# Plain float32 products for the first S5 layer's input and gate projections in a hybrid trunk

## The chip, the cores and the metric

The kernel runs on one core of one Trainium2 chip. The metric is device microseconds of one execution. The engines are TensorE (PE: matmuls, and PEld: its weight loads), VectorE (DVE), ScalarE (ACT), GpSimd (POOL) and SyncE (SP, which here only issues DMAs). TensorE's clock is granted by a throttle; the profile shows it as a share of its full 2.4 GHz.

## The reference

One inference step of a trunk of four layers: S5, retention, Hyena, S5. There are 128 context tokens and 256 latent tokens, T = 384 together, and 1024 features. Each layer is a normalisation with a modulation (shift, scale, gate computed from the condition vector with a weight of 1024 x 3072 per layer), a mixer, and a gated residual add. The change concerns the first S5 layer:

```python
def s5_branch(h, h0, w_in, ..., w_glu, b_glu, w_out):
    proj = h @ w_in                          # 1024 -> 2048
    u, gate = proj[..., :S5_WIDTH], proj[..., S5_WIDTH:]
    y = d_skip * uf + <both directions of the scan over u, 64 groups of 16 channels>
    g = jax.nn.gelu(y)
    y = g * jax.nn.sigmoid(g @ w_glu + b_glu)
    out = (y * jax.nn.silu(gate)) @ w_out
```

All inputs and outputs are float32.

## The kernel before

Activations lie feature-major: 8 blocks of 128 features by 384 tokens. A dense product is a loop over slabs of weight (1024 x 256 numbers, 1 MB), each of two blocks of 128 output features, each of which sums over the 8 input blocks: 8 positions of 128x128x384 to an output block. The input projection of layer 0 has four slabs (64 positions), and the gate projection four (slabs 4 to 7 of the same weight, 64 positions).

Precision comes from a split. `unit` (L158) makes from a raw weight block (tile `wr`) a high part `wh` by a cast on ACT (L164) and the rest `wl` by a subtraction, which `sub_any` (L146) deals to POOL (through L136) or DVE (L151) by a counter and the current share. Activations are split likewise into `hh` and `hl` by `put` (L176: cast L177, subtraction L178). `mm` (L138) then issues three products for each position, high by high, high by low and low by high, each in a reduced float32 type. If its operands come unsplit, it issues one plain float32 product.

The raw weights of all these products come through one pool of two buffers (`weight`, L153, tag `wr`), loaded over SP's queue. The modulation weights of the coming layers use the same two buffers: each layer has 12 slabs of 1 MB, and a unit (`mod_unit`, L369, its products at L381) loads one and multiplies it by the condition vectors. Units are queued and taken one by one by `tick` (L355) between other work.

The S5 layer (`s5`, L701) goes through a list of steps written as a string:

```python
PLAN0 = "A7 U0 T1 U1 T1 P0 A9 T1 P1 A11 T1 U2 T1 P2 A13 T1 P3 A15 T1 R0 U3 T1 P4 T1 A16 P5 T1 T1 P6 P7 R1"
```

U is one slab of the input projection (its result goes through memory into tile `U`, L769 and L770). A builds scan weights ahead on DVE from small tables (`gen_b1`, L642; L631, L632, L636). For six of the sixteen blocks this also builds a weight `CP` that is needed later and spilled to memory: two DVE products per direction (L631, L632), an adding DMA from POOL's queue (L634) and a store from that queue (L650); one buffer serves all six, so one spill's build waits for the store of the spill before. P (`use_p`, L742) multiplies `U` by the built scan weights (L749) and transposes (L758). R is the recurrence over chunks (L795 to L798 on DVE, R0 and R1 for two halves of the groups). T is a tick.

After the plan the gate projection follows, held back until the last product of the last P has been issued. Then the groups: the kernel matrices are loaded from memory in eight small DMAs each (tile `Tt`, L852) and transposed (L857), products of `U` and of the recurrence's states `X` give y (L884), and GELU follows. The result is split into `g_parts` (`gh`, `gl`), which the GLU projection reads. A tile scheduler that simulates times fixes the order of each engine's instructions from this program and from the pools.

Of the kernel before, what the change touches and what calls it, by code (L numbers as in the profile page):

```python
# [10 lines left out]
F32 = mybir.dt.float32  # L11
F32R = mybir.dt.float32r
# [6 lines left out]
NB = D // 128  # L19
# [88 lines left out]
def hybrid_trunk(ctx: ExitStack, tc: tile.TileContext, I, O, dbg=None, layers=(0, 1, 2, 3)):  # L108
# [62 lines left out]
    def parts_tile(pool, nb, name):  # L171
        if not SPLIT:
            return [pool.tile([128, nb, T], F32, name=name)]
        return [pool.tile([128, nb, T], F32R, tag=name + s, name=name + s) for s in ("h", "l")]
# [5 lines left out]
    def featmajor(raw, act, nkb, epi, base=0):  # L180
        for m in range(raw.shape[2] // 128):
            ps = psd()
            for k0 in range(0, nkb, NB):
                w = unit(raw[:, k0:k0 + NB, m * 128:(m + 1) * 128])
                for kb in range(NB):
                    mm(ps[:, :T], [p[:, kb, :] for p in w], [a[:, k0 + kb, :] for a in act],
                       k0 + kb == 0, k0 + kb == nkb - 1)
            epi(base + m, ps[:, :T])
# [171 lines left out]
    def drain():  # L360
        tick(len(bg))

    macc = [None, True]

    def settle():
        while not macc[1]:
            tick()

    def mod_unit(i, s, pool=None):  # L369
        if pool is None:  # L370
            raw = weight(I["mod_w"][i, s])
        else:
            raw = load(pool, "wm", I["mod_w"][i, s], tag="wm")
        u, g = s % 4, s // 4
        if u == 0:
            macc[0] = psn()
        ps, macc[1] = macc[0], u == 3
        for k2 in range(2):
            for q in range(4):
                kb = q * 2 + k2  # L380
                TE.matmul(ps[q * 32:(q + 1) * 32, :256], sg[:, kb, 6 - 2 * u:38 - 2 * u], raw[:, kb, :],  # L381
                          start=u == 0 and k2 == 0, stop=u == 3 and k2 == 1)
        if u < 3:
            return
        row = tmp.tile([128, 256], F32, tag="mrow", name="mrow", bufs=1)
        S.copy(row, ps[:, :256])
        for b in range(2):
            TE.matmul(ps[:, 256 + 8 * b:264 + 8 * b], row[:, b * 128:(b + 1) * 128], sel, start=True, stop=True)
        if g == 0:
            MODS[i] = tuple(cst.tile([128, n, 2], F32, name=f"{nm}{i}") for nm, n in (("mod", 24), ("sc", NB), ("gt", NB)))  # L390
        m, sc, gt = MODS[i][:3]
        mb = vec[:, V_MODB + i * 24 + 8 * g:V_MODB + i * 24 + 8 * g + 8].rearrange("p (u b) -> p b u", b=2)
        V.tensor_add(m[:, 8 * g:8 * g + 8, :].rearrange("p (u b) r -> p b u r", b=2),
                     ps[:, 256:272].rearrange("p (b u r) -> p b u r", b=2, u=4),
                     mb.unsqueeze(3).to_broadcast([128, 2, 4, 2]))
        if g == 1:
            V.scalar_tensor_tensor(sc, m[:, 8:16, :], 1.0,
                                   vec[:, V_G + i * 8:V_G + i * 8 + 8].unsqueeze(2).to_broadcast([128, NB, 2]),
                                   op0=OP.add, op1=OP.mult)
            MODS[i] += (True,)  # L400
        if g == 2:
            V.tensor_scalar(gt, m[:, 16:24, :], GT_F[i], None, op0=OP.mult)
# [50 lines left out]
    def adanorm(i, actp, eng=V):  # L453
        m, sc, gt = MODS[i][:3]
        rb, marks = rstd_bcast()
        h = parts_tile(actp, NB, "h")
        early = EARLY.get(i)
        if early:
            early.rb, early.marks = rb, marks
        for fb in range(NB):  # L460
            t = t384("ht")
            mul = V.tensor_mul(t, (early.x[fb] if early else xT[:, fb, :])[:, :T], rb[:, :T])
            if fb == AM:
                ADA[0] = mul.ins
            if early:
                for v, (a, b) in enumerate(SEGS):
                    hi, bias = h[0][:, fb, a:b], m[:, fb, v:v + 1]
                    if fb in HP:
                        G.tensor_scalar(hi, t[:, a:b], bias, None, op0=OP.add)
                    else:  # L470
                        S.activation(hi, t[:, a:b], AF.Identity, bias=bias)
                    V.scalar_tensor_tensor(h[1][:, fb, a:b], t[:, a:b], bias, hi.bitcast(F32), op0=OP.add, op1=OP.subtract)  # L472
                continue
            f = t384("hf")
            for v, (a, b) in enumerate(SEGS):
                S.activation(f[:, a:b], t[:, a:b], AF.Identity, scale=sc[:, fb, v:v + 1], bias=m[:, fb, v:v + 1])
            put(h, fb, f, eng=eng)
        return h

    class Early:  # L480
# [220 lines left out]
    def s5(i, j, nxt, begun=lambda: None):  # L701
# [28 lines left out]
        PBs = {}  # L730
        mark = [None]
        if j == 0:
            grot = mk(eP, "s5g", 2)

        def get_p(hb):
# [75 lines left out]
        for op in (PLAN0, PLAN1)[j].split():  # L811
# [13 lines left out]
            else:  # L825
                tick(n)
        pool_share[0] = PSG
        eP.close()
        if j == 0:
            eT.close()  # L830
# [8 lines left out]
        if j == 1:  # L839
            while gates:  # L840
                gates.popleft()()
        g_parts = [hpool.tile([128, NB, T], F32R, tag="h" + q, name="g" + q) for q in "hl"]
        e2 = ExitStack()
        rot = mk(e2, "s5c", 2)
        Tms = {}
# [732 lines left out]
```

## Time and profile before

| | us |
|---|---|
| median of 3 runs | 1631.56 (1630.19 to 1633.90) |
| profiled execution | 1632.28 |
| its span in the trace | 1630.5 |
| busy PE / DVE / ACT / POOL | 1449.2 / 1246.0 / 692.2 / 664.3 |
| mean granted clock | 0.951 |

The profile is of one execution; its own time is 1.8 us above its span and 0.7 us above the median. Layer 0 takes the first quarter of it. The busy times are sums over stages of very different limits, so what follows is read stage by stage: windows of busy time, and in each the instructions that start late.

### The profile page before, as it was taken

Reading aid. Unit: us, or ns where it says so; the run is one execution under the profiler, and the core shown is the slowest. Engines: PE = TensorE matmul, PEld = TensorE weight load, DVE = VectorE, ACT = ScalarE, POOL = GpSimd, SP = SyncE. Lnnn points to the kernel's source line nnn. Section 1 sums busy time; section 2 is a strip of 40 time slices with the busy share of each in tenths; the row PEclk is TensorE's granted clock in tenths of the full one; section 3 lists DMA queues with packets and bytes.
Section 4 is the critical chain, followed back from the end, with each engine's and each line's share of the span. In section 5 each row is a group of like instructions: output and inputs, shape, how many; then the busy total and the mean of one; then the engine's idle time right before and its main releaser. Section 6 shows DMA issues by size and latency. Waiting matters only on the chain. (4 is left out here: it accounts for less than half of the span.)

```text
span 1630.5 us, 27608 instructions
## 1 busy us (share of the span) xinstructions
PE 1449.2 (89%) x10370; PEld 1280.7 (79%) x10370; DVE 1246.0 (76%) x2935; ACT 692.2 (42%) x1275; POOL 664.3 (41%) x484
## 2 busy tenths in 40 slices
PE   6778787798799899999979999999999999988996
PEld 3555585577588888889968988999998898767886
DVE  8966998699886767755968887888888874379565
ACT  2434522244333333334445544546445534542443
POOL 2111242325374857551225665655666332132221
PEclk9887899899799999999989999999999999999998
DMA  9487499843555555543333322322322345577531
GB/s 359 130 260 224 150 222 253 284 178 128 216 173 179 183 207 187 183 154 130 127 125 101 101 78 75 101 84 95 100 78 94 106 174 201 167 217 196 199 130 65
DMA packets 107805, 261.39 MB, mean 160 GB/s; under 512 B 28535, under 2 KB 68568, under 8 KB 88088
## 3 DMA queue, kind: packets, MB, share of 16 engines
q1 hardware_dynamic: 80768, 200.12, 37.2%
q0 software_dynamic: 11984, 34.87, 7.7%
q10 hardware_dynamic: 14920, 24.65, 4.3%
q8 instruction: 82, 1.34, 0.3%
q14 instruction: 51, 0.42, 0.1%
HBM read 220.37 MB, written 30.83 MB: 154 GB/s over the span
## 5 line engine op out<-in xcount | busy, mean ns | idle before, releaser
L136 POOL TENSOR_TENSOR wl<-wr,wh 128x1024 fp32r<-128x1024 f32 (+2 forms) x99 | 248.9, 2515 | 300.2 <-ACT wh L164 273.6
L164 ACT CAST wh<-wr 128x1024 fp32r<-128x1024 f32 (+4 forms) x211 | 215.7, 1028 | 315.0 <-PE psd L141 200.5
L141 PE MATMUL psd<-hh,wh 128*128 128x384 f32 x880 | 307.3, 350 | 13.5 <-DVE X L798 7.0
L141 PE MATMUL psd<-hl,wh 128*128 128x384 f32 x880 | 305.7, 347 | 6.4 <-DVE hl L472 6.2
L141 PE MATMUL psd<-hh,wl 128*128 128x384 f32 x880 | 305.3, 347 | 4.7 <-POOL wl L136 2.6
L151 DVE TENSOR_TENSOR wl<-wr,wh 128x1024 fp32r<-128x1024 f32 (+3 forms) x112 | 147.2, 1315 | 71.9 <-ACT wh L164 71.5
L141 PEld LDWEIGHTS psd<-hh,wh 128*128 128x128 f32 x880 | 169.7, 193 | 26.6 <-issue 14.5
L141 PEld LDWEIGHTS psd<-hl,wh 128*128 128x128 f32 x880 | 169.9, 193 | 15.9 <-DVE hl L472 8.9
L141 PEld LDWEIGHTS psd<-hh,wl 128*128 128x128 f32 x880 | 169.7, 193 | 12.2 <-issue 5.1
L141 PE MATMUL psd<-wl,hh 128*128 128x256 f32 x384 | 110.0, 288 | 4.0 <-POOL wl L136 2.0
L141 PE MATMUL psd<-wh,hh 128*128 128x256 f32 x384 | 110.0, 292 | 2.6 <-ACT k L1077 1.6
L141 PE MATMUL psd<-wh,hl 128*128 128x256 f32 x384 | 109.0, 286 | 0.0
L381 PE MATMUL psn<-wr,sgc 128*32 128x256 f32 x640 | 58.3, 460 | 35.0 <-DMA wr<-in_mod_w_dram 23.9
L141 PE MATMUL psd<-zb,wh 128*128 128x384 f32 x240 | 80.9, 338 | 0.0
L141 PEld LDWEIGHTS psd<-wl,hh 128*128 128x128 f32 x384 | 74.1, 193 | 6.3 <-POOL wl L136 3.2
L141 PEld LDWEIGHTS psd<-wh,hh 128*128 128x128 f32 x384 | 73.3, 193 | 4.5 <-ACT k L1077 2.0
L636 POOL TENSOR_TENSOR BP<-BP,xt 128x512 f32<-128x512 f32 x32 | 47.3, 1479 | 71.9 <-DVE xt L632 36.4
L141 PEld LDWEIGHTS psd<-wh,hl 128*128 128x128 f32 x384 | 74.1, 193 | 0.1
L631 DVE TENSOR_TENSOR CP<-B,xc 128x512 f32<-128x512 f32 x52 | 52.9, 1044 | 26.5 <-DMA scratch_cpd_dram<-CP 15.6
L632 DVE TENSOR_TENSOR xt<-BI,xc 128x512 f32<-128x512 f32 x52 | 47.2, 909 | 29.6 <-POOL CP L636 17.2
L381 PEld LDWEIGHTS psn<-wr,sgc 128*32 128x32 f32 x640 | 20.0, 124 | 56.9 <-DMA wr<-in_mod_w_dram 27.8
L797 DVE TENSOR_TENSOR X<-X,m 128x64 f32<-128x64 f32 x184 | 64.2, 349 | 0.0
(385 smaller groups left out, 3843.1 us busy)
## 6 DMA issues: line engine op xcount, KB each, us to landing
wr<-in_mod_w_dram SPq DMA_DIRECT2D x40, 1024.0 KB
wr<-in_hy_w_in_dram SPq DMA_DIRECT2D x32, 1024.0 KB
wr<-in_ret_w_in_dram SPq DMA_DIRECT2D x24, 1024.0 KB
wr<-in_s_w_in_dram SPq DMA_DIRECT2D x16, 1024.0 KB
wm<-in_mod_w_dram SPq DMA_DIRECT2D x8, 1024.0 KB
CP<-xt POOLq DMA_DIRECT2D x32, 256.0 KB, 7.2
Tt<-scratch_kd_dram SPq DMA_DIRECT2D x128, 64.0 KB
wr<-in_s_w_glu_dram SPq DMA_DIRECT2D x8, 1024.0 KB
```

What stands on the lines that cost most here:

```text
L136: G.tensor_tensor(out, a, b, op=op)
L141: TE.matmul(out, lhs[a], rhs[b], start=start and i == 0, stop=stop and i == len(combos) - 1)
L151: V.tensor_sub(out, a, b)
L164: S.copy(hi, ap)
L381: TE.matmul(ps[q * 32:(q + 1) * 32, :256], sg[:, kb, 6 - 2 * u:38 - 2 * u], raw[:, kb, :], start=u == 0 and k2 == 0, stop=u == 3 and k2 == 1)
L631: eng.tensor_tensor(out, c1, x[:, 0].unsqueeze(2).to_broadcast([128, 4, 8, 16]), op=OP.mult)
L632: eng.tensor_tensor(t, c2, x[:, 1].unsqueeze(2).to_broadcast([128, 4, 8, 16]), op=OP.mult)
L636: add.tensor_tensor(out, out, t, op=OP.add)
L797: V.tensor_add(dst, dst, m1[:, 0])
```

## The change

For layer 0 the activations `h` become one plain float32 tile (name `hf`, tag `hh`), written directly by ACT, with no `put`. The products of the input and gate projections take the raw weight `wr` as it was loaded, with no `unit`. While the pools of the plan are open (`eP`), modulation units load into a buffer of their own (pool "s5m", tag `wm`, one buffer); afterwards they share `wr` again. The low half of `g_parts` of layer 0 takes its space from another pool. `featmajor` chooses by the number of activation parts, so other layers and the GLU keep their split.

```diff
@@ featmajor
-                w = unit(raw[:, k0:k0 + NB, m * 128:(m + 1) * 128])
+                w = raw[:, k0:k0 + NB, m * 128:(m + 1) * 128]
+                w = unit(w) if len(act) > 1 else [w]
@@
-    macc = [None, True]
+    macc, mpool = [None, True], [None]
@@ mod_unit
+        pool = pool or mpool[0]
         if pool is None:
             raw = weight(I["mod_w"][i, s])
         else:
@@ adanorm
-        h = parts_tile(actp, NB, "h")
+        h = parts_tile(actp, NB, "h") if i else [actp.tile([128, NB, T], F32, tag="hh", name="hf")]
@@
-            f = t384("hf")
+            f = t384("hf") if i else h[0][:, fb, :]
             for v, (a, b) in enumerate(SEGS):
                 S.activation(f[:, a:b], t[:, a:b], AF.Identity, scale=sc[:, fb, v:v + 1], bias=m[:, fb, v:v + 1])
-            put(h, fb, f, eng=eng)
+            if i:
+                put(h, fb, f, eng=eng)
@@ s5
         if j == 0:
+            mpool[0] = mk(eP, "s5m")
             grot = mk(eP, "s5g", 2)
@@
         pool_share[0] = PSG
+        mpool[0] = None
         eP.close()
@@
-        g_parts = [hpool.tile([128, NB, T], F32R, tag="h" + q, name="g" + q) for q in "hl"]
+        g_parts = [(rpool if j == 0 and q == "l" else hpool).tile([128, NB, T], F32R, tag="h" + q, name="g" + q) for q in "hl"]
```

The scheduler orders the program anew. Two places matter. The rows give the line of each version's own file (the changed one is up to five lines longer), the operation, output and inputs, the tile's shape and, after the x, how many follow one another.

The first place is TensorE's order at the end of the gate projection. Before, the last products of slab 7 stand ahead of the modulation units (`wr,sgc`), the transposes of `Tt` and the first group's products (`Tm,U`):

```order
L141 MATMUL psd<-hh,wh 128x384
L141 MATMUL psd<-hl,wh 128x384
L141 MATMUL psd<-hh,wl 128x384
L381 MATMUL psn<-wr,sgc 32x256 x8
L857 MATMUL psm<-ident,Tt 128x128 x8
L884 MATMUL psm<-Tm,U 64x128 x4
L857 MATMUL psm<-ident,Tt 128x128 x4
L381 MATMUL psn<-wr,sgc 32x256 x8
```

With the change, the second half of slab 4 to slab 6 and what stands between them on TensorE:

```order
L141 MATMUL psd<-hf,wr 128x384 x6
L383 MATMUL psn<-wr,sgc 32x256 x8
L390 MATMUL psn<-sel,mrow 128x8 x2
L141 MATMUL psd<-hf,wr 128x384 x16
L383 MATMUL psn<-wr,sgc 32x256 x8
L862 MATMUL psm<-ident,Tt 128x128 x16
L141 MATMUL psd<-hf,wr 128x384 x16
L383 MATMUL psn<-wr,sgc 32x256 x8
L862 MATMUL psm<-ident,Tt 128x128 x16
L889 MATMUL psm<-Tm,U 64x128 x2
L889 MATMUL psm<-CP,X_200 48x128 x4
```

The first group's products have moved ahead of slab 7 (whose 16 products follow some rows on), and each slab's 16 products stand in one piece.

The second place is SP's queue from the last slabs of the plan into the gate projection. Before:

```order
L155 DMA wr<-in_s_w_in_dram 128x2048
L155 DMA wr<-in_mod_w_dram 128x2048
L155 DMA wr<-in_s_w_in_dram 128x2048
L852 DMA Tt<-scratch_kd_dram 16x8x128 x8
L155 DMA wr<-in_mod_w_dram 128x2048
L852 DMA Tt<-scratch_kd_dram 16x8x128 x3
L155 DMA wr<-in_s_w_in_dram 128x2048
L852 DMA Tt<-scratch_kd_dram 16x8x128 x5
```

With the change:

```order
L132 DMA wm<-in_mod_w_dram 128x2048 x5
L857 DMA Tt<-scratch_kd_dram 16x8x128 x7
L155 DMA wr<-in_s_w_in_dram 128x2048
L155 DMA wr<-in_mod_w_dram 128x2048
L857 DMA Tt<-scratch_kd_dram 16x8x128 x9
L692 DMA xc<-in_s5bc_dram 128x256 x4
L874 DMA CP<-scratch_cpd_dram 128x1024 x2
L155 DMA wr<-in_s_w_in_dram 128x2048
L692 DMA xc<-in_s5bc_dram 128x256
L155 DMA wr<-in_mod_w_dram 128x2048
```

The `in_s_w_in` loads of the first fence are slabs 4, 5 and 6, those of the second are slabs 5 and 6. Slab 5 has moved behind five modulation weights and seven loads of `Tt`, and loads of spilled weights (`CP`) have moved ahead of slab 6.

## Rows read from the trace of the kernel before

**Rows 1.** Page: the span, then one group: count | busy, mean ns | idle.

```profile
span 1630.5 us, 27608 instructions
...
L797 DVE TENSOR_TENSOR X<-X,m 128x64 f32<-128x64 f32 x184 | 64.2, 349 | 0.0
```

**Rows 2.** Windows of layer 0; columns in the first row, counts in brackets.

```profile
core 0: us, PE busy (x) PEld busy (x) DVE busy (x) ACT busy (x) POOL busy (x), PEclk, DMA share, GB/s
54.00:99.00 45.00, 43.01 (x316) 34.26 (x316) 36.82 (x70) 24.07 (x55) 5.35 (x7) 0.94 0.71 215
99.00:195.80 96.80, 68.40 (x661) 43.15 (x660) 71.39 (x231) 42.06 (x88) 17.13 (x19) 0.77 0.73 220
195.80:245.00 49.20, 44.53 (x285) 40.83 (x284) 47.23 (x232) 15.23 (x25) 17.96 (x10) 0.93 0.77 188
245.00:334.00 89.00, 63.10 (x710) 47.87 (x713) 65.21 (x240) 24.64 (x48) 24.55 (x26) 0.88 0.89 259
262.00:310.00 48.00, 32.32 (x394) 23.59 (x392) 31.68 (x101) 13.24 (x27) 12.73 (x14) 0.86 0.99 291
334.00:420.00 86.00, 73.41 (x462) 62.87 (x462) 76.84 (x191) 32.78 (x55) 28.86 (x27) 0.98 0.45 165
```

**Rows 3.** Tiles wh and hl, layer 0: ns min/median/max, first and last start us, forms.

```profile
L164 ACT CAST wh<-wr x14: 1040/1045/1076, 71.2 to 230.6; 128x1024 fp32r<-128x1024 f32 x14
L136 POOL TENSOR_TENSOR wl<-wr,wh x8: 2331/2432/2733, 171.7 to 237.7; 128x1024 fp32r<-128x1024 f32 x8
L151 DVE TENSOR_TENSOR wl<-wr,wh x6: 1216/1218/1224, 73.5 to 125.1; 128x1024 fp32r<-128x1024 f32 x6
...
L178 DVE TENSOR_TENSOR hl<-hf,hh x8: 545/548/550, 54.2 to 67.4; 128x384 fp32r<-128x384 f32 x8
```

**Rows 4.** TensorE's timeline: start us, us, instruction xcount [idle before it, releaser].

```profile
202.12 0.33 PE L141 MATMUL psd<-hh,wl 128*128 128x384 f32 x1
202.29 0.33 PE L141 MATMUL psd<-hh,wh 128*128 128x384 f32 x1
...
234.39 0.66 PE L141 MATMUL psd<-hh,wh 128*128 128x384 f32 x1 [2.02 <-DVE X L798]
...
240.29 0.37 PE L141 MATMUL psd<-hh,wh 128*128 128x384 f32 x1
...
1396.04 2.76 PE L498 MATMUL psd<-xb,wr 128*128 128x386 f32 x8
```

**Rows 5.** POOL's timeline at the first gate slab's subtractions.

```profile
171.68 5.03 POOL L136 TENSOR_TENSOR wl<-wr,wh 128x1024 fp32r<-128x1024 f32 x2 [10.02 <-ACT wh L164]
```

**Rows 6.** DVE's timeline: recurrence steps, the last spill's build, the last step.

```profile
172.27 2.23 DVE L797 TENSOR_TENSOR X<-X,m 128x64 f32<-128x64 f32 x1
...
177.60 1.28 DVE L631 TENSOR_TENSOR CP<-B,bc 128x512 f32<-128x512 f32 x2
...
180.55 0.21 DVE L797 TENSOR_TENSOR X<-X,m 128x64 f32<-128x64 f32 x1
...
295.41 0.21 DVE L798 TENSOR_TENSOR X<-X,sw 128x64 f32<-128x64 f32 x1
```

**Rows 7.** SP's timeline: issue of gate slabs 6 and 7.

```profile
209.21 0.34 SPq L155 DMA_DIRECT2D wr<-in_s_w_in_dram  x1
...
223.12 0.33 SPq L155 DMA_DIRECT2D wr<-in_s_w_in_dram  x1
```

**Rows 8.** ACT's timeline: the casts that wait for these slabs.

```profile
217.25 1.99 ACT L164 CAST wh<-wr 128x1024 fp32r<-128x1024 f32 x2 [5.32 <-DMA wr<-in_s_w_in_dram]
...
229.67 1.99 ACT L164 CAST wh<-wr 128x1024 fp32r<-128x1024 f32 x2 [4.12 <-DMA wr<-in_s_w_in_dram]
```

**Rows 9.** TensorE's timeline: first gate product, a modulation unit, first GLU product.

```profile
195.83 0.44 PE L141 MATMUL psd<-hh,wh 128*128 128x384 f32 x1
...
302.50 1.07 PE L381 MATMUL psn<-wr,sgc 128*32 128x256 f32 x16 [2.70 <-DMA wr<-in_mod_w_dram]
...
330.71 0.62 PE L141 MATMUL psd<-gh,wh 128*128 128x384 f32 x2 [0.94 <-ACT gh L177]
```

## The prediction, made before the changed kernel had run

> **What bounds the kernel now.** I read the span first [rows 1], then the table of windows around layer 0 [rows 2], which the change alone touches; later layers keep their instructions. The layer runs through three limits. From 99 to 195.8 us TensorE is busy 68.4 of 96.8 us at a clock of 0.77, so it waits; DVE, with 71.4, builds the scan's weights and spills some of them to memory, and the products with those weights (use_p) come at that pace. From the first gate product at 195.83 [rows 9] to 245 TensorE is busy 44.5 of 49.2 and DVE 47.2: gate projection and recurrence lie side by side. From 245 to the first GLU product at 330.71 [rows 9] TensorE is busy 63.1 of 89 and the DMA engines 0.89, from 262 to 310 even 0.99 at 291 GB/s [rows 2]; a modulation weight keeps TensorE waiting there (2.70 us at 302.50 [rows 9]), and the last recurrence step comes only at 295.41 [rows 6]. So the casts that go were hardly a limit by themselves, the subtractions were, and the raw gate weights will be.
>
> **Matmul price.** A split product takes 0.173 us (the next one starts at 202.29 after 202.12 [rows 4]), so a 128x128x384 position costs 3 x 0.173 = 0.52. A plain float32 product of 386 columns stands in layer 3: 8 instructions in 2.76 us, two to a position [rows 4]. The last one counts to its end, about 0.49, so the pitch is (2.76 - 0.49)/7 = 0.325 and a position costs 0.65. The change adds 0.13 us x 64 = 8.3 us to each projection, 16.6 in all; no PE time is saved. The Trainium skill, FP8 and Floating Point Precision, section TensorE Precision Notes, counts four passes for true FP32 against one for the reduced format; by it a position would rise by a third, 0.69 us, and the projections by 22 us. The row gives a quarter, and the row is used.
>
> **What is removed.** Sixteen ACT casts of 1.045 us, eight DVE subtractions of 1.218 for the input weights, eight POOL subtractions of 2.43 for the gate weights, and eight DVE subtractions of 0.548 on the activations [rows 3] with their casts. The ACT time lies beside other work (42.1 of 96.8 us busy [rows 2]) and counts as nothing; if that cover were gone it would be worth at most the 1 us lead of the first cast. The two kinds on DVE make 8 x 1.218 + 8 x 0.548 = 14.1 us, all before 126 us. The POOL ones cost more than their own time: at 171.68 two of them run for 5.03 us [rows 5], and the recurrence additions on DVE beside them take 2.23 us where the same addition takes 0.21 at 180.55 [rows 6]. That is 2.0 us of DVE per POOL subtraction; over the whole profile this line averages 349 ns [rows 1]. The Trainium skill, SBUF — State Buffer, section Who interferes with whom, has the reason, one port pair that DVE and GpSimd share under an exclusive lock. The pair at 171.68 sits just ahead of the last spilled weight's build, 177.60 [rows 6], on which the last use_p waits.
>
> **Up to the first gate product.** Without that pair the build starts 2 x 2.02 = 4.0 us earlier. Of the 14.1 us taken off DVE I count 1: DVE is 82% busy from 54 to 99 (36.8 of 45), but the builds also wait on their own stores. Against it stand 8.3 us more of input products. In the order all of them come before the first use_p, and TensorE's 28 idle us of 99 to 195.8 lie behind them; what that idle time doesn't take up moves the end. The modulation weights get one buffer of their own where they shared two with the slabs, so a load there waits for the unit ahead. A unit is 1.07 us [rows 9] and a load some 7 (below), 8.1 together; 11 ticks in 141.8 us stand 12.9 apart on average, so I take nothing, but the last five are queued on SP in a row, ahead of the kernel-table loads Tt and gate slab 5, and five units at 8.1 us apart cost TensorE some of its idle time. Value -5; bounds -7 (the pair, and 3 of the 14.1) and +8 (all of the extra input products, or one late load, on the path).
>
> **From there to the GLU.** The gate weights now stay in their buffer until the matmuls have read them; before, cast and subtraction freed it. The two buffers of wr alternate between slab and modulation weight. In the order SP issues slab 5, a modulation weight, slab 6, a modulation weight, slab 7; slab 6 gets the buffer of slab 5. So the load of each of slabs 5 to 7 starts when the slab ahead is consumed, and TensorE has only a modulation unit and 16 transposes to do meanwhile. Issue to cast took 217.25 - 209.21 = 8.0 us and 229.67 - 223.12 = 6.5 [rows 7, 8], so 7.3. A slab is 16 x 0.65 = 10.4 us of products. After a wait of 2.02 us TensorE came back at the lower clock level (1.2 GHz): a product lasts 0.66 us at 234.39 instead of 0.33, and 0.37 again only at 240.29 [rows 4]. Half of those 6 us are lost, 3. So: slab 4, 10.4 + 1 for the transposes of use_p among it; then three times 7.3 + 13.4; 73.5 us where 49.2 are now. The tail shrinks in return, because modulation units, transposes and the first half of a group go into the waits. Of its 23.1 MB (89 us at 259 GB/s [rows 2]) two modulation slabs and a GLU slab (1.05 MB each), two loads of spilled weights (0.52 each), eight Tt (0.06 each) and four accumulations (0.26) fall on the other side by the order: 5.7 MB, and 17.4 are left. At 291 GB/s that is 59.8 us, at the mean 259 it is 67.2. First gate product to first GLU product is then 73.5 + 59.8 = 133.3 against 134.9 now, so -1.6. The recurrence isn't in the way: the six POOL subtractions from here on go, 6 x 2.0 = 12 us, and it ends 99.6 - 12 = 87.6 us after the first gate product. Bounds: -9, where the recurrence sets the end (87.6 + the 35.3 that follow it now = 122.9, a few us of loads on top), and +8, with the loads at 8.0 and the tail at 259 GB/s (75.6 + 67.2 = 142.8).
>
> **GLU and after.** Two modulation units move into the GLU stage, where TensorE is busy 73.4 of 86 us: 2 x 1.07 = 2.1, of which I take 1 (0 to 2). The half of g_parts that gets another pool is first written with the first group, when that space has long been free: nothing. The counter that deals subtractions between POOL and DVE runs 16 calls behind afterwards; that changes which of two engines takes one, and I take nothing, with 2 either way.
>
> Sum: -5 - 1.6 + 1 = -5.6 on the profiled execution's 1632.28 us (0.7 above the median) gives 1626.7; against the median, 1626.
>
> **Rivals.** *The recurrence sets the tail*: DVE is freed by 12 us, transfers get hidden in the waits, and the GLU starts 126 us after the gate; 126 - 134.9 - 5 + 1 = -13, some 1618. For it speaks that DVE is busy 47.2 of 49.2 us there; against it, that TensorE's order is fixed and gate slabs come late. *The bytes set the end*: from gate to GLU all but two of the same slabs have to come, and what the start gains is waited out at 0.99 busy; -2 to +3, some 1631. *Exposed gate loads win*: the waits of slabs 5 to 7 are not paid back. At 142.8 us the stage loses 7.9; with the start's gain down to 2 this is 7.9 - 2 + 1 = +7, some 1639. It decides as soon as the stretch from gate to GLU exceeds 134.9 + 4 = 139 us. For it: loads of 8 us between 10.4 us slabs can't hide in two buffers. Against: modulation work fills part of the wait, and slower gates leave DMA engines room. *TensorE sets the pace* throughout: all 16.6 us show, some 1649. Against this speak its 28 + 26 idle us (96.8 - 68.4, 89 - 63.1 [rows 2]). The skill's four passes belong here, with 1654.
>
> **How the numbers follow.** Forecast 1622 to 1628.3: 0.29. Recurrence, 1611 to 1622: 0.18. Bytes, 1628.3 to 1634.8: 0.20. Exposed loads, 1634.8 to 1646: 0.26. TensorE's pace, 1646 and above: 0.07. The range 1611 to 1646 leaves out 0.07 and the ends of the outer cases. 0.2% is 3.3 us, about what a measurement can tell here: faster 0.47, same 0.20, slower 0.33. Within the faster cases alone the time is 1611 to 1628.
>
> **What would show it.** The first gate product near 191 us and no DVE addition above 1 us beside it in the recurrence; the products of slabs 5, 6 and 7 each start behind a wait of 5 to 8 us for a DMA of wr; last gate product 73 us after the first; recurrence over about 88 us after it; first GLU product 133 us after it. I am wrong if plain products run at another pitch than 0.325 us, if input products delay the first gate product, or if the GLU starts over 139 us behind the gate.

## The result and the profile after

The changed kernel takes 1673.95 us (median of 4 runs, 1661.84 to 1680.69) against 1632.39 before: ratio 1.0255, 95% interval 1.0224 to 1.0285. It is 41.6 us slower. The forecast was 1626 in a range of 1611 to 1646, so the range and the sign were both wrong.

The page of the changed kernel has a span of 1669.1 us, 38.6 longer than that of [rows 1]. Of its engines (busy us, share, instructions) TensorE is the busiest, and its work grew by 28 us (1449.2 before), more than the 16.6 of the dearer products:

```profile
PE 1477.6 (89%) x10242; PEld 1279.6 (77%) x10242; DVE 1234.0 (74%) x2917; ACT 678.3 (41%) x1251; POOL 647.5 (39%) x478
```

Here are the windows of layer 0 that answer [rows 2], cut at the marks of this run: first gate product to last, to the last cast of `gh`, to the last product of the output projection. Columns as in [rows 2].

```profile
192.20:265.00 72.80, 57.57 (x280) 34.52 (x280) 57.08 (x346) 11.04 (x21) 8.70 (x10) 0.91 0.73 187
265.00:342.10 77.10, 54.25 (x595) 42.55 (x595) 36.89 (x94) 22.89 (x45) 16.26 (x18) 0.75 0.78 227
342.10:429.50 87.40, 80.07 (x481) 72.51 (x480) 78.17 (x202) 31.76 (x54) 31.28 (x29) 0.94 0.49 175
```

The same three stretches in a second execution of the kernel before (run e13, below, span 1632.4 us):

```profile
191.90:240.70 48.80, 42.62 (x290) 38.13 (x292) 44.59 (x210) 15.31 (x25) 18.42 (x10) 1.00 0.75 186
240.70:329.10 88.40, 63.14 (x700) 49.23 (x701) 64.11 (x240) 24.16 (x48) 23.55 (x25) 0.84 0.90 261
329.10:408.40 79.30, 72.00 (x424) 63.71 (x422) 71.34 (x166) 32.20 (x53) 29.86 (x28) 0.96 0.41 148
```

The gate stage grew by 24 us, the tail behind it shrank by only 11, and the GLU with the output projection grew by 8: that is 21 us against e13, and 18 against the first trace of before, of the 37 and 39 by which the spans differ. The rest, 16 and 21, comes later. Lay equal instructions of the first traces of before and after side by side, and the distance between them stays between 12 and 22 us, mostly near 16, from the end of layer 0 to 1300 us, through retention and most of Hyena. It then rises to 38 between 1310 and 1450 us, at the end of the Hyena layer, where the change edits nothing.

Over the gate stage and the tail together TensorE was busy 57.57 + 54.25 = 111.8 of 149.9 us, and 42.62 + 63.14 = 105.8 of 137.2 in e13. So its busy time grew by 6 us and its idle time by 7. In the GLU stage it is busy 8 us longer, which is the whole of that stage's growth.

### The profile page after: what moved, and what is told of

The parts are those of the page before. It is cut to its first block, busy times and chain, and to the rows that moved or that the text cites. A ratio compares the mean times of both kernels' runs of the same rounds, so it can differ in the third digit from the quotient of the medians.

```text
span 1669.1 us, 27271 instructions
## 1 busy us (share of the span) xinstructions
PE 1477.6 (89%) x10242; PEld 1279.6 (77%) x10242; DVE 1234.0 (74%) x2917; ACT 678.3 (41%) x1251; POOL 647.5 (39%) x478
## 5 line engine op out<-in xcount | busy, mean ns | idle before, releaser
L136 POOL TENSOR_TENSOR wl<-wr,wh 128x1024 fp32r<-128x1024 f32 (+3 forms) x93 | 233.0, 2506 | 317.0 <-ACT wh L164 302.3
L164 ACT CAST wh<-wr 128x1024 fp32r<-128x1024 f32 (+4 forms) x195 | 199.4, 1027 | 306.9 <-PE psd L141 193.1
L141 PE MATMUL psd<-hh,wh 128*128 128x384 f32 x752 | 260.9, 348 | 6.3 <-DVE X L802 3.7
L141 PE MATMUL psd<-hl,wh 128*128 128x384 f32 x752 | 258.6, 344 | 6.2 <-DVE hl L474 6.1
L141 PE MATMUL psd<-hh,wl 128*128 128x384 f32 x752 | 260.2, 347 | 1.0 <-DVE wl L151 0.6
L141 PEld LDWEIGHTS psd<-hl,wh 128*128 128x128 f32 x752 | 144.3, 192 | 12.7 <-DVE hl L474 8.5
L141 PEld LDWEIGHTS psd<-hh,wl 128*128 128x128 f32 x752 | 144.2, 192 | 8.5 <-issue 5.1
L141 PE MATMUL psd<-hf,wr 128*128 128x384 f32 x256 | 92.3, 518 | 13.9 <-DMA wr<-in_s_w_in_dram 13.9
L141 PEld LDWEIGHTS psd<-hf,wr 128*128 128x128 f32 x256 | 50.7, 203 | 50.6 <-DMA wr<-in_s_w_in_dram 14.5
L637 POOL DMA_DIRECT2D CP<-xt x32 | 28.2, 938 | 125.4 <-DVE X L802 41.7
L634 DVE TENSOR_TENSOR BP<-F,bc 128x512 f32<-128x512 f32 x64 | 59.0, 931 | 21.7 <-PE psm L677 18.5
```

The source lines that it names most:

```text
L136: G.tensor_tensor(out, a, b, op=op)
L141: TE.matmul(out, lhs[a], rhs[b], start=start and i == 0, stop=stop and i == len(combos) - 1)
L164: S.copy(hi, ap)
L634: eng.tensor_tensor(out, c1, x[:, 0].unsqueeze(2).to_broadcast([128, 4, 8, 16]), op=OP.mult)
L637: nc.gpsimd.dma_start(out, t, accum_op=OP.add)
```

## The experiments

Most of what follows compares marks in the traces, so they stand here together. All are start times in us, but for the third column, which is an end. "First gate to it" runs from the first gate product to the last cast of `gh`, and the text below calls it the stretch. "Layer 0 out" is the last output-projection product of layer 0, and the last column is the span minus that, which is everything after layer 0. Each row is one execution, where the times in the text are medians.

| run | first gate | last gate (end) | last recurrence step | last cast of gh | first gate to it | first GLU | last GLU | layer 0 out | rest |
|---|---|---|---|---|---|---|---|---|---|
| before | 195.8 | 245.3 | 295.4 | 332.4 | 136.6 | 312.5 | 366.9 | 411.6 | 1218.9 |
| before again (e13) | 191.9 | 240.7 | 292.5 | 329.1 | 137.2 | 309.2 | 363.6 | 408.4 | 1224.0 |
| after | 192.2 | 265.0 | 276.3 | 342.1 | 149.9 | 339.2 | 381.7 | 429.5 | 1239.6 |
| after again (e14) | 193.7 | 265.3 | 277.3 | 340.1 | 146.4 | 337.3 | 379.8 | 427.2 | 1240.3 |
| e1 after, dealt as before | 193.7 | 265.7 | 276.5 | 340.0 | 146.3 | 338.0 | 380.7 | 428.7 | 1218.3 |
| e2 before, dealt as after | 192.0 | 240.6 | 292.5 | 330.2 | 138.2 | 308.9 | 369.0 | 412.1 | 1243.0 |
| e3 input only | 192.7 | 242.4 | 299.9 | 338.1 | 145.4 | 327.8 | 372.6 | 416.9 | 1215.2 |
| e4 gate only | 195.8 | 269.9 | 280.0 | 344.5 | 148.7 | 338.1 | 380.6 | 429.2 | 1220.6 |
| e5 no units between slabs | 194.3 | 237.0 | 275.3 | 338.2 | 143.9 | 322.6 | 372.0 | 421.2 | 1224.7 |
| e6 no modulation buffer | 194.6 | 270.3 | 295.5 | 339.9 | 145.3 | 333.2 | 376.4 | 425.2 | 1223.9 |
| e7 subtractions on DVE | 192.6 | 246.3 | 301.6 | 339.0 | 146.4 | 327.4 | 374.8 | 422.7 | 1219.7 |
| e8 gate weights copied | 199.4 | 247.8 | 289.8 | 348.5 | 149.1 | 328.6 | 383.1 | 432.9 | 1221.0 |
| e9 after, no units to GLU | 196.4 | 239.1 | 290.8 | 326.5 | 130.1 | 286.3 | 362.1 | 410.5 | 1244.9 |
| e10 before, no units to GLU | 193.6 | 242.5 | 297.9 | 324.8 | 131.2 | 282.3 | 359.9 | 406.9 | 1244.4 |
| e11 tables on POOL's queue | 194.9 | 267.9 | 278.6 | 354.7 | 159.8 | 324.1 | 388.9 | 434.2 | 1221.4 |
| e12 before, third dealing | 189.0 | 237.7 | 288.8 | 325.6 | 136.6 | 305.9 | 358.7 | 402.8 | 1244.3 |
| e15 GLU slab ahead | 194.6 | 267.8 | 279.1 | 340.0 | 145.4 | 332.1 | 375.4 | 424.2 | 1225.7 |

A difference of less than 7 us in the mark of the first gate product means nothing: in before, e2, e12 and e13 the instructions up to there are the same and stand in the same order, and it lies between 189.0 and 195.8.

### The dealing of subtractions

A counter deals each subtraction of a split to POOL or DVE, by its remainder modulo 3. The change leaves out 16 calls, one more than a multiple of 3, so every later subtraction falls on another turn. Two runs take this apart.

```diff
 # e1: the changed kernel
                 w = unit(w) if len(act) > 1 else [w]
+                flip[0] += len(act) == 1
 # e2: the kernel before
+        if j == 0:
+            flip[0] += 2
         g_parts = [hpool.tile(...) for q in "hl"]
```

e1: 

> The changed kernel, except that the counter that deals subtractions between POOL and DVE still counts each omitted split, so that every later subtraction is dealt to the engine it had before. The time against before came in two steps: some 17 us by the end of layer 0 and some 20 more between 1320 and 1450 us, where no instruction was edited. Theory (the dealing): the second step comes from the shifted counter; this run then takes about 1632 + 17 = 1649 us (1645 to 1655), and the steps past 1300 us line up with before. Rival (the new order and its other side effects, not the dealing): the second step stays, 1665 to 1680 us.

e2: 

> The kernel before, with the counter moved by two ahead of the groups of layer 0, which shifts the dealing of every later subtraction as the 16 omitted calls of the change do (16 is 1 more than a multiple of 3). Nothing else. Theory (the dealing): 1632 + 20 = about 1652 us, lost between 1320 and 1450 us. Rival (other side effects): within 3 us of 1632.

e1 took 1650.58 us (ratio 1.0117, 1.0085 to 1.0148), e2 1658.67 (1.0166, 1.0124 to 1.0207), against 1629.18 for before. Both follow the theory, though e2 lost 29 us where 20 were expected. In the last column of the table e1 is back among the runs of before, at 1218, and e2 leaves them, at 1243. So about 20 us of the loss (41.6 without the count kept, 21.4 with it) is a side effect: no product was made dearer, some subtractions changed engines in layers that the change doesn't touch, and the scheduler ordered those layers anew.

Where the time goes shows in windows that begin at about the same place in the Hyena layer and end at layer 3's first norm, in e13 (first line) and e2 (second):

```profile
1290.00:1385.80 95.80, 88.45 (x544) 83.78 (x544) 61.95 (x90) 40.57 (x71) 26.78 (x28) 0.98 0.50 182
1293.90:1403.90 110.00, 96.44 (x563) 90.35 (x561) 64.93 (x94) 41.57 (x72) 26.53 (x27) 0.93 0.45 164
```

e2 needs 14 us more there: TensorE is idle 13.6 us instead of 7.4, and at a granted clock of 0.93 instead of 0.98 it is busy 8 us longer. Its longest wait but for the norm's own (3.63 us, in e13 3.85), in e2 and, by the second fence, the same in the changed kernel, is one for a DVE product of the Hyena gating (`ac`), after which the products `zhh,wh` run at the lower clock level (0.52 us each, 0.34 at full clock):

```profile
1313.76 0.83 PE L1256 MATMUL psm<-ident,ac 128*128 128x128 f32 x3 [3.48 <-DVE ac L1298]
1318.80 0.52 PE L141 MATMUL psd<-zhh,wh 128*128 128x384 f32 x1
```

```profile
1327.89 0.53 PE L1259 MATMUL psm<-ident,ac 128*128 128x128 f32 x3 [3.47 <-DVE ac L1301]
```

In e1 and in both runs of before, that wait isn't there. Why the other order was chosen, and the 5 us that come after layer 3's norm, I did not resolve.

The third dealing asks whether only the change's dealing is bad. The edit is `flip[0] += 1` at the place of e2.

e12: 

> The kernel before with the counter moved by one, not two, ahead of the groups of layer 0: the third of the three ways in which the later subtractions can fall on POOL and DVE. Theory (the dealing before happens to suit this order, and any other loses): 1640 to 1660 us. Rival (only the dealing that the change makes is bad, by a collision at the end of the Hyena layer): within 4 us of 1629.

1656.13 us (1.0156, 1.0107 to 1.0206), 1244 us behind layer 0: the third dealing loses as much. It doesn't lose it in one place. By equal instructions beside the first trace of before, e12 is 9 us ahead at the end of layer 0, 2 behind at 1250 us, 12 behind at 1400 and 17 at the end, and the wait for `ac` isn't in it. So of the three dealings that of before is the fast one here, and the other two pay 24 and 29 us; that every place at which the count shifts would cost as much is not shown.

### The two projections apart

```diff
 # e3: the kernel before, input projection only
-                firstmajor(i, weight(I["s5_w_in"][j, n]), h, u_epi, 2 * n)
+                firstmajor(i, weight(I["s5_w_in"][j, n]), [h[0].bitcast(F32)] if j == 0 else h, u_epi, 2 * n)
 # e4: the kernel before, gate projection only
-            dense(I["s5_w_in"][j, 4:8], 4, h, NB, gate_epi, TG)
+            dense(I["s5_w_in"][j, 4:8], 4, [h[0].bitcast(F32)] if j == 0 else h, NB, gate_epi, TG)
```

Both also have `featmajor` leave such weights unsplit and keep the count of the counter.

e3: 

> The kernel before with plain float32 products for the input projection of layer 0 alone, on the high half of the activations (the low half is left out of these products); gate projection split as before, modulation weights share the two buffers, the counter counts as before. Theory (the gate projection's waits make the loss in layer 0): first gate product within 4 us of 195.8 and the total within 5 us of 1632. Rival (the input products are the loss): over 1640 us.

e4: 

> The kernel before with plain float32 products for the gate projection of layer 0 alone, on the high half of the activations (the low half is left out); input projection split, modulation weights share the two buffers, the counter counts as before. Theory (slabs that hold their buffer until the matmuls have read them): gate stage some 70 us long with waits of 3 to 11 us for slabs 5 to 7, first GLU product some 10 to 25 us later than before, total 1643 to 1652 us. Rival (the loss needs the input side or the modulation buffer too): within 4 us of 1632.

e3 took 1638.99 us (1.0052, 1.0031 to 1.0073, 10 runs) and e4 1640.38 (1.0065, 1.0035 to 1.0095, 10 runs). By medians that is +9.8 and +11.2, together 21.0, and e1, which has both, has +21.4. The marks don't add up like that, for the trace of e3 is of the fastest of its ten executions (1633.94) and that of e4 of the second slowest (1651.56), with its layer 0 as long as e1's. So the agreement of the sum may be chance. e3 lies outside what its theory allowed (within 5 us) and short of what its rival asked (over 1640): its first gate product stays where it was, but the stretch to the last cast of `gh` grew to 145.4 us though nothing in it was edited. e4 behaves as its theory said for the gate stage (74 us), and its median is 2.6 us below the band for the total.

### What stretches the part from gate to GLU

TensorE's timeline in the changed kernel, the gate slabs alone (columns as in [rows 4]):

```profile
192.24 6.72 PE L141 MATMUL psd<-hf,wr 128*128 128x384 f32 x20
199.81 4.14 PE L141 MATMUL psd<-hf,wr 128*128 128x384 f32 x12
209.04 12.11 PE L141 MATMUL psd<-hf,wr 128*128 128x384 f32 x32 [2.99 <-DMA wr<-in_s_w_in_dram]
234.95 12.80 PE L141 MATMUL psd<-hf,wr 128*128 128x384 f32 x32 [10.91 <-DMA wr<-in_s_w_in_dram]
254.45 10.59 PE L141 MATMUL psd<-hf,wr 128*128 128x384 f32 x32
```

and SP's queue beside it:

```profile
203.97 0.35 SPq L155 DMA_DIRECT2D wr<-in_s_w_in_dram  x1
...
224.98 0.49 SPq L155 DMA_DIRECT2D wr<-in_s_w_in_dram  x1
...
249.29 0.38 SPq L155 DMA_DIRECT2D wr<-in_s_w_in_dram  x1
```

As the forecast had it, each slab is loaded when the slab ahead has been read (slab 6 is issued at 224.98, behind the end of slab 5 and two more loads, and lands ten us later). But is that the loss? Four runs ask, all on e1's version except e7. Of e8's edit the switch is left out that keeps the copy to the gate projection.

```diff
 # e5: no unit between gate slabs
-            dense(I["s5_w_in"][j, 4:8], 4, h, NB, gate_epi, TG)
+            dense(I["s5_w_in"][j, 4:8], 4, h, NB, gate_epi, 0 if j == 0 else TG)
 # e6: no buffer of their own for modulation weights
-            mpool[0] = mk(eP, "s5m")
 # e7: the kernel before, gate subtractions on DVE
-        pool_share[0] = PSG
+        pool_share[0] = PSG if j else 0
 # e8: raw gate weights copied by ACT, products read the copy
+                    c = wsp.tile([128, 1024], F32R, tag="wh", name="wh")...bitcast(F32)
+                    S.copy(c, w)
+                    w = [c]
```

e5: 

> The changed kernel with subtractions dealt as before, and with no modulation unit queued between the gate slabs of layer 0 (they come later, with the groups and the GLU). The two buffers of wr then go from slab to slab, and slab 6 can load while slab 5 is read. Theory (the slab that waits for the slab ahead of it stretches the gate stage): no wait over 2 us for a gate slab but the first, gate stage about 45 us where it is 73, first GLU product 5 to 15 us sooner, total 1638 to 1646 us against 1650.6 for the changed kernel with this dealing. Rival (the loss lies in the groups' tail, where all loads share one queue, whatever the gate stage does): gate stage shorter, tail longer by as much, total 1648 to 1655 us.

e6: 

> The changed kernel with subtractions dealt as before, without the modulation weights' own buffer: units share the two buffers of wr throughout, as before the change. Theory (this buffer neither costs nor brings much, since TensorE waits for the scan's weights in that stage anyway): within 4 us of 1650.6. Rival (the five loads queued in a row on SP behind one buffer delay slab 5 and the kernel tables): 5 us or more faster, 1645 us or less.

e7: 

> The kernel before with the eight gate subtractions of layer 0 on DVE (1.22 us each) in place of POOL (2.43 us each); later subtractions dealt as before. It takes the POOL subtractions from beside the recurrence and leaves everything else. Theory (what the change gains comes from these eight): first gate product 3 to 4 us sooner, the recurrence's end 2 to 10 us sooner (12 us less standing still, 9.8 us of subtractions more), total 1624 to 1630 us. Rival (they cost nothing that matters): 1629 to 1634 us, or slower since DVE is the busier engine.

e8: 

> The changed kernel with subtractions dealt as before, and with each raw gate weight block copied by ACT into one of two further buffers, from which the plain products read: ACT's part of the split comes back (1.05 us each), the subtraction doesn't, and a slab's buffer is free as soon as it is copied. Theory (holding the buffer until the matmuls have read it is the loss): no wait over 4 us for gate slabs, gate stage 45 to 58 us, total 1636 to 1646 us. Rival (the dearer products or the loads themselves are the loss): 1648 to 1655 us.

e5 took 1648.88 us (1.0102, 1.0062 to 1.0142), and here the rival holds. The waits for slabs are gone, and the gate stage is, with that of e9, the shortest of all, 42.7 us, with 108 of its 128 products in one piece:

```profile
201.88 35.10 PE L141 MATMUL psd<-hf,wr 128*128 128x384 f32 x108
```

Yet the last cast of `gh` comes 143.9 us after the first gate product, only 2.4 us sooner than in e1. The theory is right on one mark: the first GLU product comes 15 us sooner (322.6 against 338.0) and layer 0 ends 7.5 us sooner, but the part behind layer 0 is 6.4 us longer. e8 points the same way, though it also puts eight copies on ACT: the gate stage is 48 us, as in before, and the stretch is 149.1 and the total 1655.99 (1.014, 1.0093 to 1.0187). So the slab that waits for its buffer is real and doesn't set the end of the stretch. e6, 1651.91 (1.0128, 1.0081 to 1.0176), shows that the modulation weights' own buffer neither costs nor saves, within what can be told.

e7 is the surprise: 1648.61 us (1.0095, 1.0063 to 1.0127), although it keeps every product split and takes the POOL subtractions from beside the recurrence. The additions that stood still are back at their price, as the first line (e7) shows against the second (e13):

```profile
L797 DVE TENSOR_TENSOR X<-X,m x92: 208/220/228, 167.9 to 301.0; 128x64 f32<-128x64 f32 x92
```

```profile
L797 DVE TENSOR_TENSOR X<-X,m x92: 201/209/2986, 165.0 to 291.0; 128x64 f32<-128x64 f32 x92
```

but the recurrence ended 109.0 us after the first gate product instead of 99.6 to 100.6, with 9.8 us of subtractions added to the same engine. What the change gains on the recurrence (84 us) goes with leaving the subtractions out; moving them gained nothing.

That leaves the loads of the tail. Between the first gate product and the GLU stand 12 modulation units, which serve later layers. e9 (on e1's version) and e10 (on before) move them behind it, so that two units are left in the stretch, and e11 moves the table loads from SP's queue to POOL's.

```diff
 # e9, e10
+            dense(..., 0 if j == 0 else TG)
-                tick(CT)
+                tick(CT if j else 0)
 # e11
-                nc.sync.dma_start(Tt[16 * t:16 * t + 16], src)
+                (nc.sync if j else nc.gpsimd).dma_start(Tt[16 * t:16 * t + 16], src)
```

e9: 

> The changed kernel with subtractions dealt as before and no modulation unit between the first gate product and the GLU of layer 0: four units between gate slabs and eight among the groups are taken later (they serve layers 2 and 3). That takes 12 loads of 1 MB and 12.8 us of TensorE from the stretch that grew from 136.6 us (first gate product to last cast of gh) to 146. Theory (in this stretch all loads stand in SP's one queue and move at under 300 GB/s, so bytes and stalls of that queue set its end): the stretch shrinks by 15 to 35 us, total 1620 to 1640 us. Rival (the chain of products, transposes and gelu over the groups sets it, whatever is loaded): the stretch shrinks by under 5 us, total 1647 to 1660 us, since the units cost TensorE later.

e10: 

> The kernel before with the same edit, the control for the run above: no modulation unit between the first gate product and the GLU of layer 0. Theory (bytes and stalls of SP's queue set the end of this stretch here too): the stretch of 136.6 us shrinks by 10 to 30 us, total 1605 to 1625 us. Rival (the recurrence, 99.6 us after the first gate product, and the 37 us behind it set it): shrinks by under 5 us, total 1628 to 1640 us.

e11: 

> The changed kernel with subtractions dealt as before, its 64 loads of the kernel tables Tt in layer 0 issued from POOL's queue instead of SP's. The bytes are the same; what waits behind them on SP (gate slabs, modulation weights, GLU slabs) no longer waits for a buffer of Tt to come free. Theory (stalls of SP's queue): waits for gate slab 6 and for the first GLU slab shrink, last cast of gh 5 to 12 us sooner, total 1638 to 1646 us against 1650.6. Rival (bytes): the same time within 3 us, 1648 to 1654 us; or slower, if the tables now wait behind the adding DMAs on POOL.

For the stretch the theory of e9 holds: it falls from 146.3 to 130.1 us. In e10 it falls by 5.4, less than forecast. Without these units both versions need the same, 130 and 131 us. So the plain products as such cost nothing there; with the units in it, the changed version pays 16 us for them and before pays 5 to 6. Two windows of the stretch, e1 (first line) and e9 (second), say of what the 16 us consist:

```profile
193.70:340.00 146.30, 106.44 (x867) 73.72 (x866) 92.95 (x437) 33.83 (x66) 25.94 (x29) 0.87 0.78 213
196.40:326.50 130.10, 97.78 (x734) 72.63 (x733) 95.86 (x440) 33.35 (x64) 27.26 (x30) 0.85 0.68 166
```

TensorE is busy 8.7 us less and idle 7.6 us less, so both the units' own products and the waiting that comes with them are in it; the runs don't part their loads from their products. Against before, e1's stretch is longer by idle time alone: by the same kind of window before is busy 106.1 of 136.6 us.

The totals, 1660.06 (1.019, 1.0142 to 1.0239) and 1653.83 (1.0153, 1.0117 to 1.0189), are above what either theory had for e10, and at the upper end of the rival's for e9: behind layer 0 both lose 20 to 27 us. They lose it in the retention layer, where some 13 units are now multiplied between the end of layer 0 and 720 us, and 3 were. So a shift of the dealing is not the only edit that costs this much in later layers. e11 took 1656.44 (1.0156, 1.0115 to 1.0196) and put the stretch up to 159.8: the tables now wait on POOL's queue for the adding DMAs (`CP<-xt`) to land, up to 4.79 us at a time. Moving one queue's load to another was no cure here.

### The GLU's weights, and second executions

In the changed kernel the GLU starts late. SP's queue behind the gates:

```profile
309.01 7.98 SPq L155 DMA_DIRECT2D wr<-in_mod_w_dram  x3
332.37 0.33 SPq L155 DMA_DIRECT2D wr<-in_s_w_glu_dram  x1
```

TensorE's waits in the tail:

```profile
272.90 1.32 PE L383 MATMUL psn<-wr,sgc 128*32 128x256 f32 x16 [2.40 <-DMA wr<-in_mod_w_dram]
...
293.29 1.94 PE L383 MATMUL psn<-wr,sgc 128*32 128x256 f32 x16 [4.27 <-DMA wr<-in_mod_w_dram]
299.75 1.94 PE L862 MATMUL psm<-ident,Tt 128*128 128x128 f32 x8 [4.53 <-DMA Tt<-scratch_kd_dram]
...
325.20 0.67 PE L889 MATMUL psm<-CP,X 128*48 128x128 f32 x4 [4.63 <-DMA CP<-xt]
...
339.22 0.69 PE L141 MATMUL psd<-gh,wh 128*128 128x384 f32 x1 [5.14 <-ACT wh L164]
```

Modulation weights hold both buffers of `wr` until their units' turn on TensorE, which stands behind groups. The last two units are multiplied at 330.92; the first GLU slab is issued at 332.37 where before had it at 303.63, and the GLU's first product waits for its cast. The wait at 325.20 is of another kind, for an adding DMA of POOL's queue. e15 puts the load of the GLU slab ahead of the last pair of groups. e13 and e14 are before and after once more.

```diff
 # e15
+            if j == 0 and m == 6:
+                pre.append(weight(I["s5_w_glu"][j, 0]))
```

e13: 

> The kernel before unchanged, for a second profile of it. The run with only the later dealing changed had its first gate product 3.8 us sooner than the first profile of before, with the same order of instructions up to there. Theory (that is the spread between executions): first gate product between 191 and 195 us here. Rival (the first profile is typical): 195.3 to 196.3 us.

e14: 

> The changed kernel unchanged, for a second profile of it. First gate product 191 to 197 us (192.2 in its first profile, 193.7 to 199.4 in four relatives with the same order up to there), last cast of gh 144 to 152 us after it, against 136.6 in the first profile of before. If the stretch is below 140 us, the first profile was an outlier.

e15: 

> The changed kernel with subtractions dealt as before, the first GLU slab's load placed ahead of the last pair of groups, where modulation weights held both buffers of wr until 332 us and the first GLU product waited until 339. Theory (the GLU starts late because its weights come late, and the output projection inherits it): first GLU product before 325 us, end of GLU 4 to 8 us nearer to the last cast of gh, total 1642 to 1648 us. Rival (the buffer taken from the modulation weights delays the groups by as much): 1649 to 1656 us.

e15: the load is issued at 311.75 and the GLU ends 35.4 us behind the last cast of `gh`, not 40.7, so the theory is right on the mechanism (the first GLU product, at 332.1, came later than its 325). But the total is 1652.7 (1.012, 1.0085 to 1.0156), no gain over e1: the 4.5 us saved in layer 0 are given back at the start of layer 1, whose order differs again. e13 (1634.17 us, one run) has its first gate product at 191.9, so the 195.8 of the first profile was late within the spread. e14 (1669.29 us, one run) repeats the changed kernel's marks within 2.3 us, apart from the stretch to the last cast of `gh`, which is 146.4 instead of 149.9.

No version was found that beats the kernel before.

## Why the prediction was wrong, step by step

| term | forecast | measured |
|---|---|---|
| up to the first gate product | -5 | about +1 (192.2, 193.7 against 189.0 to 195.8) |
| gate stage | 73.5 us | 72.8 and 71.6 |
| recurrence's end after the first gate product | 87.6 us | 84.1 and 83.6 |
| tail, bytes | 17.4 MB | 17.5 MB (77.1 us at 227 GB/s) |
| tail, time (to the last cast of `gh`) | 59.8 us | 77.1 and 74.8 |
| GLU and output projection | +1 | +8 |
| later layers | 0, 2 either way | +16 to +21 (1239.6, 1240.3 against 1218.9, 1224.0) |

**The matmul price was right.** The forecast pitch was 0.325 us. 24 input products of e14 take 8.01 us, which by the same working is (8.01 - 0.49)/23 = 0.327:

```profile
68.60 8.01 PE L141 MATMUL psd<-hf,wr 128*128 128x384 f32 x24
```

**Up to the first gate product** the sign was wrong, or at least nothing was gained. The subtractions beside the recurrence did go, and so did the long additions of [rows 1] and [rows 6]; all 92 of e14 lie between 207 and 220 ns:

```profile
L801 DVE TENSOR_TENSOR X<-X,m x92: 207/214/220, 175.5 to 277.0; 128x64 f32<-128x64 f32 x92
```

The error was to count the pair at 171.68 as ahead of the last spill's build at 177.60 [rows 5, 6]. In e13, with the same order on each engine, the build starts before the pair does:

```profile
167.15 1.29 DVE L631 TENSOR_TENSOR CP<-B,bc 128x512 f32<-128x512 f32 x2 [0.83 <-DMA scratch_cpd_dram<-CP]
```

```profile
168.64 4.98 POOL L136 TENSOR_TENSOR wl<-wr,wh 128x1024 fp32r<-128x1024 f32 x2 [10.95 <-ACT wh L164]
```

There two products `m<-X,A` behind the build stood still instead (4.80 us, where two take 0.48). So those 4.0 us were an accident of one execution. Against that, the first product with built scan weights came 12 to 14 us later (117.7 and 118.9, against 105.7 and 104.8), which TensorE's idle time took up nearly whole, as the forecast said it could.

**Gate stage, recurrence and the tail's bytes** came out near the forecast, the gate stage in part by luck. From the end of one slab's products to the next slab's it was 5.1, 13.8 and 6.7 us, not 7.3 each: 25.6 in all where 21.9 were forecast, of which 2.99 and 10.91 were waits for a slab and the rest units, transposes and a group's products. The three slabs' products took 35.5 us instead of 40.2. The two errors nearly cancelled.

**The tail's time is the first mis-sized term.** The rate was taken from the best 48 us of before, 291 GB/s at a DMA share of 0.99 [rows 2], and even the bound of 259 was too high: it was 227 to 235 GB/s at a share of 0.78 to 0.82. The share of before did not hold under another order of loads. By taking the tail as bytes over a rate, the forecast left TensorE, with 54 us of work there as measured, 6 us of idle time. It had 23 (77.1 - 54.25), about as much as the tail of e13 (88.4 - 63.14 = 25): work left the tail, and the waits did not. The five waits above make 21 of these 23 us. Four of them, 16 us, are for loads of SP's queue. That queue waited 25 us in all for units' products from 190 to 345 us here, but 32 in e13 from 190 to 331, so buffers that units hold are no new cost; which load stands behind them is, and that is seen for the GLU's first slab. e5 and e9 show that the gate's length has little to do with the stretch and the units much.

**The GLU is the second.** The row that the forecast called the first GLU product, 330.71 [rows 9], is one that waits for the last `gh` but one; the first GLU product of before is at 312.53, and 36 products, twelve positions, stand ahead of that row. The row was picked by its wait and not by its being first. So 18 us in which groups and GLU overlap were not seen, and the change loses most of them: its GLU begins 3 us ahead of the last cast of `gh`, and TensorE is busy 8 us longer behind that cast.

**The counter is the third, and as large as the others together.** The forecast saw that it runs 16 calls behind, said that this "changes which of two engines takes one", and gave it 2 us either way. It is worth some 20 us in the changed kernel (e1), and 29 and 24 in the kernel before (e2, e12). The step that failed was to price a moved subtraction by the difference of two engines, where the order of a whole layer hung on it.

By its own sign the forecast was wrong: the GLU starts 147.0 and 143.6 us behind the gate, over the 139 that it named. That was also the condition of the rival of exposed gate loads, but its reason is not what the runs show: the waits of slabs 5 to 7 can be taken away (e5, e8) and the stretch stays long. Its price was short too, 7 us for what is 9 to 13, with 8 more in the GLU. That TensorE's pace would give 1649 agrees with e1's 1650.58 by chance: the extra 16.6 us of products are not the loss, since e9 has them all and e10 has none, both without the units, and their layer 0 ends at 410.5 and 406.9.

What stays open: why every edit in this part that leaves units among the groups (e3 and e7 change neither the gate's products nor the units) takes 144 us or more for the stretch that needs 137 in before. The runs show that the units, by their loads or their products, go with it; they don't show which place in the order does it. So the 21 us of layer 0 are located, but their cause is argued and not shown. The other pool for the low half of `g_parts` was not tested by itself; e3 and e7 do without it, and their stretch is as long.

## What to carry to other kernels

An edit that leaves out calls of something counted, such as a round robin between engines, changes all that comes after it: keep the count, or measure that part alone, before the edit itself is judged. Where a scheduler fixes the order, other edits can shift later layers by as much (e9, e10). A load rate measured under one order of a queue isn't a rate of the stage; when slabs come to hold their buffers longer, ask for each load behind them what frees its buffer, and let no idle time go from the sum without naming the wait that ends. And take the first instruction of a stage as its start, not the first that waits.

## What the runs showed of the hardware

Four executions with the same instructions in the same order (in that stretch, and not all on one chip) spread the first gate product over 189.0 to 195.8 us, 6.8 us, where whole executions spread over 10.1 when nothing is changed (before: 1626.53 to 1636.61 in 19 runs). A mark in one trace is worth no more than that, and terms below it, such as the 4.0 us here, can't be read from one.

The DVE addition that takes 0.21 us alone took up to 2.99 us beside POOL's subtraction in e13, and none took over 0.23 once the subtractions were off POOL (e7) or gone (e14).
